# A decoder layer with its call list written anew: an earlier Exp table, a later broadcast, dummy products inside norm 2

## The chip, the core and the metric

The kernel runs on one core of a Trainium2 chip. The metric is the device time of one execution in microseconds (us). The engines are PE (TensorE: matmuls, with PEld for its weight loads), DVE (VectorE), ACT (ScalarE), POOL (GpSimd) and SP (SyncE, which here only issues transfers). Each engine runs its own list of instructions in the order in which the program wrote them; semaphores make one engine wait for another.

## The reference, cut to what matters

One decoder layer on 256 tokens of width 1024, all in float32:

```
mod = c @ w_ada + b_ada                      # sh1, sc1, g1, sh2, sc2, g2
h   = rmsnorm(x, norm1_g) * (1 + sc1) + sh1  # norm 1
q, k, v, xr, gr = split(h @ w_in)            # 5 x 512 columns
attn = attention(rmsnorm(q), rmsnorm(k), v)  # 8 heads, one causal block of 256
lru  = rg_lru(causal_conv4(xr)) * gelu(gr)   # gates, decay exp(-8 r softplus(-lambda)), scan over time
x = x + g1 * (concat(rmsnorm(lru), rmsnorm(attn)) @ w_out)
h2 = rmsnorm(x, norm2_g) * (1 + sc2) + sh2   # norm 2
gate, val = split(causal_conv3(h2 @ w_up))   # 2 x 2816 columns
x = x + g2 * ((silu(gate) * val) @ w_down)
```

## The kernel before, in words

Activations lie transposed: features on the 128 partitions, tokens along the row, so a 1024-wide tensor is 8 tiles (kt 0 to 7) of 128 x 256. Every large product is done three times on halves of the numbers: a weight w is cast to a high part wh (`hi`, L158, by default on ACT) and the rest wl = w - wh (`lo`, L167, on DVE), and h likewise to hh (`h_hi`, L387) and hl (`h_lo`, L390). The product is wh hh + wh hl + wl hh, so one weight tile needs four engine steps before PE has all of it.

Weights come in tiles of 1 MB, in the order of the list `order` (L101 to L113): g1 0, lin 0, g1 1, lin 1, then ada1 and lin in turn, v, g1 2 to 5 and wo, s2, g1 6 to 9, and up and dn. There are six buffers (NW = 6): when a tile has been used for the last time (`used`, L134), the next of the list is sent for (`send`, L117), and SP issues the transfers in that order. "g1" tiles hold columns of w_ada, which PE multiplies with c in 32-column products (`m1_mm`, `g1_mm`); "ada1", "s2" and "g2" tiles hold rows, which DVE multiplies with a broadcast copy of c (`ada`, L360; cb, L185).

The stages, in order:

- Head. PE runs dummy products of an identity matrix (`warm_up`, L224) while x arrives in four pieces. ACT squares it, DVE adds, PE sums over the partitions (`x_sum`), then comes 1/rms (`norm_s`, `norm_r`) and its spread over partitions (`norm_mm`). The modulation of kt 0 and 1 goes PE, ACT, PE, DVE (`m1_mm`, `m1_row`, `m1_col`, `m1_add`). `normed` and `h_hi` then make the first hh. `sp_act` and `sp(0)` to `sp(17)` (L333 to L357) are the softplus of lambda: Abs and Exp on ACT, then a series on DVE.
- lin. 8 tiles of w_in, with outputs x (RG-LRU), g (gelu), q and k. `lin(kt, out, i)` is output out with the i-th of the three products.
- Middle. The convolution (`conv_a`, `conv_d`), the RG-LRU (`gate`, `sigm`, `decay_a`, `decay_t`, `root`, `one_more`, `recur_u`, `recur_scan`, ...), the norms of q and k (`qk_r`), attention by head (`sc`, `s_max`, `s_exp`, `p_T`, `p_copy`, `pv`), and the v products as filler on PE. `v_copy` (L582) brings v out of PSUM; `pv` needs it.
- wo. `wo(c, kt)`, the output projection; then `res`, the sums of squares of norm 2 (`res_sq`, `res_add`, `res_sum`), 1/rms, `normed(1, kt)`, and the first `up`.
- up and down. `up(f, kt)`, `gated_*(f)`, `down(f, m)` for 22 panels f. From f = 4 a plain loop (L1443) writes them.

From the head to panel 3 the order on each engine is a list of some 640 calls written by hand (L801 to L1437): the scheduler is off, so a call's place in the list is its place in its engine's queue. `table(func)` (L220) is a call that does one element of a function, so that ACT loads that function's table there; without it the load comes with the first real use.

Of the kernel before, what the change touches and what calls it, by code (L numbers as in the profile page):

```python
# [13 lines left out]
P = 128  # L14
# [54 lines left out]
def hybrid_layer(ctx: ExitStack, tc: tile.TileContext, x_d, c_d, pk_d, bd_d, ada1_d, lin_d, v_d,  # L69
# [31 lines left out]
    order = []  # L101
# [4 lines left out]
    order += [("g1", 2), ("g1", 3), ("wo", 0), ("g1", 4), ("g1", 5), ("wo", 1)]  # L106
# [693 lines left out]
    kept.enter_context(tc.manual_schedule())  # L800
    warm_up(9)  # L801
    x_sq(0)
    x_sq(1)
    consts()
    c_cols()
    x_add(0, 1)
    x_sq(2)
    x_add(0, 2)
    x_sq(3)
    x_add(0, 3)  # L810
    table(AF.Sqrt)
    warm_up(12)
# [88 lines left out]
    ada("ada1", 1, 1)
    lin(2, "q", 2)
    lin(2, "g", 2)
    h_lo(0, 2)
    ada_add("ada1", 1)
    lin(2, "g", 0)
    lo("lin", 3, 0)
    normed(0, 3)
    sp(7)
    h_hi(0, 3)  # L910
    lin(2, "g", 1)
    lin(2, "x", 1)
    lin(2, "k", 1)
    lin(2, "q", 1)
    ada("ada1", 2, 0)
    h_lo(0, 3)
    lin(3, "g", 2)
    lin(3, "g", 0)
    ada("ada1", 2, 1)
    hi("lin", 4, 0)  # L920
    lo("lin", 3, 1)
    ada_add("ada1", 2)
    lin(3, "q", 0)
    normed(0, 4)
    lin(3, "k", 1)
    h_hi(0, 4)
    lin(3, "x", 2)
    lin(3, "x", 0)
    lin(3, "x", 1)
    lin(3, "g", 1)  # L930
    lin(3, "q", 2)
    sp(8)
    lo("lin", 4, 0)
    hi("lin", 4, 1)
    h_lo(0, 4)
    hi("lin", 5, 0)
    lin(3, "k", 2)
    lin(4, "x", 0)
    ada("ada1", 3, 0)
    lin(4, "g", 2)  # L940
    c_more(2)
    lin(4, "k", 1)
    lin(3, "k", 0)
    ada("ada1", 3, 1)
    lin(4, "x", 2)
    ada_add("ada1", 3)
    normed(0, 5)
    bd_load()
    lin(3, "q", 1)
    lo("lin", 4, 1)  # L950
    h_hi(0, 5)
    lin(4, "x", 1)
    h_lo(0, 5)
    lin(4, "q", 0)
    lin(4, "g", 0)
    lo("lin", 5, 0)
    hi("lin", 5, 1)
    ada("ada1", 4, 0)
    table(AF.Gelu_apprx_tanh)
    ada("ada1", 4, 1)  # L960
    lin(4, "k", 0)
    lin(5, "g", 0)
    lin(4, "g", 1)
    lin(5, "g", 1)
    hi("lin", 6, 0)
    lin(5, "k", 1)
    sp(9)
    ada_add("ada1", 4)
    lin(4, "q", 2)
    lin(5, "x", 1)  # L970
    sp(10)
    lin(5, "q", 1)
    lo("lin", 5, 1)
    lin(5, "x", 0)
    lin(5, "k", 0)
    lin(5, "q", 0)
    lin(4, "k", 2)
    normed(0, 6)
    lin(5, "g", 2)
    lin(5, "q", 2)  # L980
    lo("lin", 6, 0)
    h_hi(0, 6)
    h_lo(0, 6)
    ada("ada1", 5, 0)
    c_more(1)
    hi("lin", 6, 1)
    lin(5, "x", 2)
    table(AF.Exp)
    lin(6, "g", 0)
    ada("ada1", 5, 1)  # L990
    table(AF.Gelu_apprx_tanh)
    ada_add("ada1", 5)
    sp(11)
    normed(0, 7)
    lin(5, "k", 2)
    hi("lin", 7, 0)
    lin(6, "q", 0)
    sp(12)
    lin(6, "x", 0)
    lin(4, "q", 1)  # L1000
    lin(6, "q", 1)
    h_hi(0, 7, 1)
    lin(6, "g", 2)
    sp(13)
    hi("lin", 7, 1)
    lin(6, "g", 1)
    h_lo(0, 7)
    lin(6, "x", 2)
    lin(6, "k", 0)
    bd_copy(1)  # L1010
    lo("lin", 7, 0)
    lo("lin", 6, 1)
    lin(6, "x", 1)
    lin(7, "x", 1)
    lin(7, "x", 2)
    lin(7, "x", 0)
    lin(7, "q", 0)
    lin(7, "g", 1)
    bd_copy(0)
    lin(6, "q", 2)  # L1020
    conv_a(2)
    conv_a(0)
    lo("lin", 7, 1)
    conv_a(1)
    conv_a(3)
    hi("v", 0, 0)
    conv_d(0)
    lin(7, "q", 2)
    lin(7, "q", 1)
    lin(7, "k", 1)  # L1030
    lin(6, "k", 1)
    lin(7, "g", 2)
    q_s(0)
    q_s(1)
    q_sq(1)
    q_sq(0)
    c_more(3)
    lin(7, "g", 0)
    gelu(0)
    lin(7, "k", 0)  # L1040
    gelu(1)
    conv_d(1)
    lin(7, "k", 2)
    lin(6, "k", 2)
    k_sq(0)
    q_sum()
    k_sq(1)
    conv_d(2)
    conv_d(3)
    k_sum(0)  # L1050
    q_row(0)
    gate(1, 0)
    k_sum(1)
    q_col()
    sigm(1, 1)
    gate(0, 0)
    qk_r(0)
    gate(1, 1)
    sigm(0, 0)
    table(AF.Sigmoid)  # L1060
    sigm(1, 0)
    qk_r(1)
    lo("v", 0, 0)
    gate(0, 1)
    g1_mm(3)
    qk_r(2)
# [493 lines left out]
```

## Time and profile before

| | us |
|---|---|
| median of 3 runs (332.19 to 333.26) | 332.77 |
| the profiled execution | 332.59 |
| its span, first to last instruction | 330.8 |
| PE busy | 320.2 (97%) |
| DVE busy | 263.0 (79%) |
| ACT busy | 194.5 (59%) |

The profiled execution is 0.18 below the median, and 1.8 of it lie outside the span. A busy PE is a PE with some matmul in flight, not a PE at its peak; what ends the idle time before an instruction stands in brackets in the rows further on. The share of 97% is an average over stages: from the fourth panel on PE never waits, and the stages before are those in which other engines can hold it up.

### The profile page before, as it was taken

Reading aid. Unit: us, or ns where it says so; the run is one execution under the profiler, and the core shown is the slowest. Engines: PE = TensorE matmul, PEld = TensorE weight load, DVE = VectorE, ACT = ScalarE, POOL = GpSimd, SP = SyncE. Lnnn points to the kernel's source line nnn. Section 1 sums busy time; section 2 is a strip of 40 time slices with the busy share of each in tenths; the row PEclk is TensorE's granted clock in tenths of the full one; section 3 lists DMA queues with packets and bytes.
Section 4 is the critical chain, followed back from the end, with each engine's and each line's share of the span. In section 5 each row is a group of like instructions: output and inputs, shape, how many; then the busy total and the mean of one; then the engine's idle time right before and its main releaser. Section 6 shows DMA issues by size and latency. Waiting matters only on the chain.

```text
span 330.8 us, 6467 instructions
## 1 busy us (share of the span) xinstructions
PE 320.2 (97%) x2608; PEld 302.6 (91%) x2608; DVE 263.0 (79%) x507; ACT 194.5 (59%) x328; POOL 4.6 (1%) x22
## 2 busy tenths in 40 slices
PE   7899999999999999899999999999999999999994
PEld 7789999767599996899999999999999999999994
DVE  2469999899999998968696788888888677685654
ACT  5635458999988245865566455464646464655520
POOL 5000000000000000000000000000000000000000
PEclk9999999999999999799999999999999999999998
DMA  7999999939355998836566557575849463300003
GB/s 224 337 405 408 410 408 422 411 136 385 131 162 206 345 407 316 348 129 254 167 223 248 174 214 264 206 293 183 323 146 364 135 242 133 129 0 2 3 0 127
DMA packets 18013, 77.89 MB, mean 235 GB/s; under 512 B 1600, under 2 KB 6336, under 8 KB 10944
## 3 DMA queue, kind: packets, MB, share of 16 engines
q1 hardware_dynamic: 17840, 77.34, 62.6%
q8 instruction: 20, 0.33, 0.4%
q10 hardware_dynamic: 144, 0.15, 0.2%
q14 instruction: 9, 0.07, 0.1%
HBM read 76.43 MB, written 1.05 MB: 234 GB/s over the span
## 4 chain that ended last, share of the span: by engine, by line
PE 69%; DVE 16%; ACT 6%; issue 3%; SPq 2%; DMA 2%; DVEq 0%; ACTq 0%
PE bank L65 68%; DVE wl L172 4%; DVE w L365 4%; DMA w<-in_dram 2%; DVE m L423 2%; ACT wh L144 1%; SPq L132 1%; DVE m L766 1%; PE bank L676 1%; DVE ht L381 1%; ACT p L670 1%; DVE m L794 1%; DVE m L458 1%; DVE wh L150 1%; SPq L181 1%
## 5 line engine op out<-in xcount | busy, mean ns | idle before, releaser
L172 DVE TENSOR_TENSOR wl<-w,wh 128x1024 fp32r<-128x1024 f32 x94 | 113.2, 1220 | 19.8 <-ACT wh L144 19.1
L144 ACT CAST wh<-w 128x1024 fp32r<-128x1024 f32 x90 | 92.1, 1043 | 43.6 <-PE bank L65 34.9
L65 PE MATMUL bank<-hh__1575,wh 128*128 128x256 f32 x352 | 71.6, 285 | 1.1 <-ACT hh__1575 L148 1.1
L65 PE MATMUL bank<-hl__1576,wh 128*128 128x256 f32 x352 | 71.7, 286 | 0.0
L65 PE MATMUL bank<-hh__1575,wl 128*128 128x256 f32 x352 | 71.6, 285 | 0.0
L65 PEld LDWEIGHTS bank<-hh__1575,wh 128*128 128x128 f32 x352 | 55.3, 193 | 1.3 <-ACT hh__1575 L148 1.3
L65 PEld LDWEIGHTS bank<-hl__1576,wh 128*128 128x128 f32 x352 | 55.6, 194 | 0.2 <-DVE hl__1576 L392 0.2
L65 PEld LDWEIGHTS bank<-hh__1575,wl 128*128 128x128 f32 x352 | 55.4, 194 | 0.2 <-DVE wl L172 0.2
L766 DVE SCALAR_TENSOR_TENSOR m<-bank,pk,m 128x255 f32<-128x255 f32 x88 | 40.4, 479 | 19.0 <-ACT m L758 17.4
L65 PE MATMUL bank<-pl,wh 128*128 128x256 f32 x176 | 49.9, 284 | 0.4 <-DVE pl L782 0.4
L65 PE MATMUL bank<-ph,wh 128*128 128x256 f32 x176 | 49.9, 284 | 0.0
L65 PE MATMUL bank<-ph,wl 128*128 128x256 f32 x176 | 49.8, 283 | 0.0
L65 PEld LDWEIGHTS bank<-pl,wh 128*128 128x128 f32 x176 | 33.8, 192 | 0.6 <-DVE pl L782 0.6
L65 PEld LDWEIGHTS bank<-ph,wh 128*128 128x128 f32 x176 | 33.8, 192 | 0.1
L65 PEld LDWEIGHTS bank<-ph,wl 128*128 128x128 f32 x176 | 33.8, 192 | 0.0
L758 ACT ACTIVATE m<-bank,pk 128x256 f32<-128x256 f32 x44 | 22.4, 558 | 18.9 <-PE bank L65 18.9
L365 DVE CUSTOM_DVE_ANT_0 w<-w,cb 128x1024 f32<-128x1024 f32 x22 | 26.3, 1218 | 0.0
L770 ACT ACTIVATE m<-m 128x256 f32<-128x256 f32 x22 | 9.2, 417 | 26.8 <-DVE m L766 26.8
L65 PE MATMUL bank<-hl_mix__1178,wh 128*128 128x256 f32 x64 | 18.3, 286 | 0.2 <-DVE hl_mix__1178 L505 0.2
L65 PE MATMUL bank<-hh_mix__1177,wh 128*128 128x256 f32 x64 | 18.4, 288 | 0.0
L65 PE MATMUL bank<-hh_mix__1177,wl 128*128 128x256 f32 x64 | 18.1, 283 | 0.0
L65 PE MATMUL bank<-hh__245,wh 128*128 128x256 f32 x96 | 14.8, 283 | 1.0 <-DVE lt L345 1.0
(176 smaller groups left out, 429.5 us busy)
## 6 DMA issues: line engine op xcount, KB each, us to landing
w<-in_dram SPq DMA_DIRECT2D x55, 1024.0 KB, 5.1
w<-in_dram SPq DMA_DIRECT2D x32, 512.0 KB, 10.1
xT<-in_dram SPq DMA_DIRECT2D x4, 256.0 KB, 4.5
cb<-in_dram SPq DMA_DIRECT2D x1, 512.0 KB, 9.7
out_dram<-m SPq DMA_DIRECT2D x4, 128.0 KB, 2.5
out_dram<-m SPq DMA_DIRECT2D x2, 256.0 KB, 2.8
m<-in_dram SPq DMA_DIRECT2D x1, 256.0 KB, 9.5
pk<-in_dram ACTq DMA_DIRECT2D x1, 145.0 KB, 4.0
```

The source lines that it names most:

```text
L65: self.nc.tensor.matmul(out, lhsT, rhs, start=left == self.n, stop=left == 1, skip_group_check=True)
L132: (q or nc.sync).dma_start(raw[key][:, c:c + n], srcs[key[0]][key[1]][:, c:c + n])
L144: nc.scalar.copy(out, in_)
L150: nc.vector.tensor_copy(out, in_)
L172: (nc.vector if e else nc.gpsimd).tensor_sub(l[:, c], raw[key][:, c], h.bitcast(F32)[:, c])
L181: nc.sync.dma_start(xT[:, 2 * i:2 * i + 2, :], x_d[:, 2 * i:2 * i + 2, :])
L365: nc.vector.tensor_tensor_reduce(v[:, a, :], v[:, a, :], cb, scale=scale, scalar=0.0, op0=ALU.mult, op1=ALU.add, accum_out=mod[:, j, kt:kt ...
L381: nc.vector.scalar_tensor_tensor(T["ht", n, kt], xT[:, kt, :], mod[:, (SC1, SC2)[n], kt:kt + 1], rep, op0=ALU.mult, op1=ALU.mult)
L423: nc.vector.scalar_tensor_tensor(xc[:, t, s:], pair(B["x", t // 2])[:, t % 2, :S - s], col(O_CW + 4 * j + t), xc[:, t, s:], op0=ALU.mult, ...
L758: nc.scalar.activation(cv[:, s, :], pair(B["up", f])[:, s, :], AF.Identity, scale=col(O_FW + 88 + i), bias=col(O_FB + i))
L766: nc.vector.scalar_tensor_tensor(cv[:, s, d:], pair(B["up", f])[:, s, :S - d], col(O_FW + 44 * j + i), cv[:, s, d:], op0=ALU.mult, op1=ALU ...
L770: nc.scalar.activation(T["cv", f][:, 2, :], T["cv", f][:, 0, :], AF.Silu)
```

## The change

Six edits and a new order.

1. ACT loads the Exp table before anything else, and `sp_act` runs as soon as the packed parameters are there, ahead of the squares of x; `sp(0)` to `sp(5)` follow on DVE ahead of the adds. The Sqrt table is loaded after the squares, as before.
2. The dummy products: 18 in one run before `x_sum` in place of 21, and 3 in place of 8 behind it. sc1's column (`m1_row`, `m1_col`, `m1_add` of part 0) is taken before sh1's products (`m1_mm(0, 1)`) are made.
3. c's broadcast is sent for after the fourth weight tile (lin 1) and not after the third.
4. g1 4 and g1 5 come ahead of wo 0 in the list of weights.
5. `keep_warm`: 5 dummy products whose result nobody reads, in two places between the sums of norm 2 and the first `up`. Beside them, `g1_mm(6)`, `(7)` and `(9)` come before the last sums and `(8)` after.
6. Some casts change engine: for example `h_hi(1, 2)` and both casts of up 4 go from ACT to DVE, and the second cast of wo 2 and one of v 0 from DVE to ACT.

The calls themselves, but for the dummy products and the `table` calls, are the same ones; lines behind L226 move by 7.

```diff
-    order += [("g1", 2), ("g1", 3), ("wo", 0), ("g1", 4), ("g1", 5), ("wo", 1)]
+    order += [("g1", 2), ("g1", 3), ("g1", 4), ("g1", 5), ("wo", 0), ("wo", 1)]
...
     for i in range(NW):
         send()
-        if i == 2:
+        if i == 3:
             nc.sync.dma_start(cb, c_d.to_broadcast([P, D]))
...
+    def keep_warm(n):
+
+        b = get(B, "idle", lambda: bank(3, 1))
+        for _ in range(n):
+            b.reopen(1)
+            b.mm(b.t[:, 0:P], ident, ident)
...
+    table(AF.Exp)
     warm_up(9)
+    sp_act()
     x_sq(0)
+    consts()
+    sp(0)
...
     norm_s("n2")
+    g1_mm(8)
+    keep_warm(2)
     g1_row(1)
     norm_r()
     g1_col(1)
+    norm_mm("n2")
+    keep_warm(3)
     lo("up", 1, 0)
-    norm_mm("n2")
     g1_add(1)
     normed(1, 2)
-    h_hi(1, 2)
+    h_hi(1, 2, 1)
```

Three places show how the lists move. The first is PE in the head, before; ident are the dummy products (and, with rms, the spread of 1/rms), ccol the columns of c, ones the column sums, and hh with wh the first product of lin:

```order
L65 MATMUL bank_147<-ident 128x128 x21
L65 MATMUL bank_185<-ones,m_157 128x2 x4
L65 MATMUL bank_199<-w,ccol 32x128 x8
L65 MATMUL bank_147<-ident 128x128 x6
L65 MATMUL bank_199<-w,ccol 32x128 x8
L65 MATMUL bank_185<-ident,rms 128x128 x2
L65 MATMUL bank_199<-ones,m_230 128x2
L65 MATMUL bank_199<-ones,m_232 128x2
L65 MATMUL bank_147<-ident 128x128 x2
L65 MATMUL bank_253<-hh__245,wh 128x256 x2
```

The same place on PE in the changed kernel:

```order
L65 MATMUL bank_148<-ident 128x128 x18
L65 MATMUL bank_191<-ones,m_160 128x2 x4
L65 MATMUL bank_205<-w,ccol 32x128 x8
L65 MATMUL bank_148<-ident 128x128
L65 MATMUL bank_205<-ones,m_214 128x2
L65 MATMUL bank_205<-w,ccol 32x128 x8
L65 MATMUL bank_191<-ident,rms 128x128 x2
L65 MATMUL bank_205<-ones,m_232 128x2
L65 MATMUL bank_148<-ident 128x128 x2
L65 MATMUL bank_253<-hh__243,wh 128x256 x2
```

Three dummy products before the sums and five behind them are gone, and one column sum stands ahead of the second group of ccol products.

The second place is ACT in the attention, before, from the first exponential on; p are the probabilities, L465 the squares of the RG-LRU output, pt copies a transposed head, m_1041 is v:

```order
L670 ACT_TABLE_LOAD
L670 ACTIVATE p,rs<-p,eb,iqk 128x128
...
L465 ACTIVATE m_885<-m_784 128x1024
L144 COPY pt<-bank_1008 128x384
...
L144 COPY m_1041<-bank_862 128x512
L144 COPY pt<-bank_1029 128x384
L144 COPY m_1041<-bank_898 128x512
```

The same stretch of ACT in the changed kernel (m_1044 is v, the casts are the two halves of wo 0's high part):

```order
L677 ACT_TABLE_LOAD
L677 ACTIVATE p,rs<-p,eb,iqk 128x128
L677 ACTIVATE p,rs<-p,eb,iqk 128x256
L144 CAST wh<-w 128x1024
...
L472 ACTIVATE m_869<-m_754 128x1024
...
L144 COPY m_1044<-bank_848 128x512
L222 ACTIVATE warm<-ones 128x1
L144 COPY row<-bank_877 128x256
L144 COPY pt<-bank_1022 128x384
L144 COPY m_1044<-bank_837 128x512
```

Before, three heads' exponentials (two rows each) stand ahead of the second copy of v; now four heads', two casts and a row copy do, while the three casts that came ahead of the table load are gone.

The third place is DVE at norm 2, before; sr are the sums of squares, xT<-bank the residual adds, hm and rms the norm, ht the first normed tiles:

```order
L740 TENSOR_TENSOR sr<-sr 128x256 x5
L732 SCALAR_TENSOR_TENSOR xT<-bank_1421,mod,xT 128x256 x2
L172 TENSOR_TENSOR wl<-w,wh 128x1024
L375 TENSOR_TENSOR mod<-mod,pk 128x2 x2
L172 TENSOR_TENSOR wl<-w,wh 128x1024
L375 TENSOR_TENSOR mod<-mod,pk 128x2
L273 TENSOR_SCALAR hm<-bank_1502 128x2
```

The same place on DVE in the changed kernel:

```order
L739 SCALAR_TENSOR_TENSOR xT<-bank_1410,mod,xT 128x256 x2
L747 TENSOR_TENSOR sr<-sr 128x256 x2
L172 TENSOR_TENSOR wl<-w,wh 128x1024
L150 CAST wh<-w 128x1024
L172 TENSOR_TENSOR wl<-w,wh 128x1024
L280 TENSOR_SCALAR hm<-bank_1521 128x2
```

Between the last residual adds and hm there are now two adds, two splits and a cast of up 1's second half, where there were two splits of up 0 and three small adds.

## Rows read from the trace of the kernel before

**Rows 1.** The page: busy times of the engines, and the granted clock over the span.
```profile
PE 320.2 (97%) x2608; PEld 302.6 (91%) x2608; DVE 263.0 (79%) x507; ACT 194.5 (59%) x328; POOL 4.6 (1%) x22
...
PEclk9999999999999999799999999999999999999998
```
**Rows 2.** PE's waits: line, waited for, total us, times, longest us.
```profile
PE bank L65 <- ACT hh__1575 L148: 1.1, 1, 1.1
...
PE bank L65 <- DVE pl L782: 0.4, 1, 0.4
```
**Rows 3.** Stretches: length; busy us of each engine; clock; DMA share; GB/s.
```profile
64.40:100.20 35.80, 35.03 (x262) 26.07 (x263) 34.14 (x102) 33.47 (x80) 0.00 (x0) 1.00 0.57 217
...
133.20:137.00 3.80, 3.77 (x17) 3.55 (x18) 3.79 (x10) 2.67 (x6) 0.00 (x0) 0.55 1.02 427
```
**Rows 4.** Timeline of the head: start us, length us, instruction, idle before it.
```profile
1.75 7.54 PE L65 MATMUL bank<-ident 128*128 128x128 f32 x42 [1.75 <-POOL ident L197]
...
6.50 1.37 ACT L305 ACTIVATE m<-xT 128x512 f32<-128x512 f32 x2 [0.44 <-DMA xT<-in_dram]
...
10.12 0.26 ACT L268 ACTIVATE rms<-bank,eps 128x2 f32<-128x2 f32 x1 [0.73 <-PE bank L65]
...
10.58 1.60 PE L65 MATMUL bank<-ident 128*128 128x128 f32 x12
...
14.37 0.48 DVE L381 SCALAR_TENSOR_TENSOR ht<-xT,mod,bank 128x256 f32<-128x256 f32 x1
...
15.45 0.71 PE L65 MATMUL bank<-hh__245,wh 128*128 128x256 f32 x4 [0.97 <-DVE lt L345]
```
**Rows 5.** Transfers issued in 4.1 to 4.3 us: KB, us to landing.
```profile
w<-in_dram SPq DMA_DIRECT2D x1, 512.0 KB, 8.1
```
**Rows 6.** Transfers issued in 8.4 to 9 us.
```profile
w<-in_dram SPq DMA_DIRECT2D x1, 512.0 KB, 10.1
```
**Rows 7.** Timeline early in the lin stage, PE.
```profile
19.50 0.65 PE L65 MATMUL bank<-w,ccol 128*32 128x128 f32 x16
```
**Rows 8.** Timeline at the end of the lin stage, ACT, DVE and PE.
```profile
52.25 1.28 ACT L222 ACT_TABLE_LOAD   x1
...
56.23 3.50 DVE L172 TENSOR_TENSOR wl<-w,wh 128x1024 fp32r<-128x1024 f32 x3
...
58.77 1.93 ACT L148 ACTIVATE m<-bank,pk 128x256 f32<-128x256 f32 x4 [0.34 <-PE bank L65]
...
64.90 0.64 PE L65 MATMUL bank<-m,sel 128*32 128x256 f32 x8 [0.50 <-ACT m L436]
```
**Rows 9.** Timeline of the middle, ACT and PE.
```profile
77.09 1.06 ACT L449 ACTIVATE m<-m 128x1024 f32<-128x1024 f32 x1
...
83.97 0.49 ACT L670 ACTIVATE p<-p,eb,iqk 128x128 f32<-128x128 f32 x1 [0.73 <-DVE eb L665]
...
89.33 0.58 ACT L144 COPY m<-bank 128x512 f32<-128x512 f32 x1
...
90.44 0.88 PE L65 MATMUL bank<-m,pt 128*128 128x64 f32 x6
...
100.22 0.37 PE L65 MATMUL bank<-hh_mix__1177,wh 128*128 128x256 f32 x1
```
**Rows 10.** Timeline of norm 2, PE.
```profile
126.39 1.93 PE L65 MATMUL bank<-w,ccol 128*32 128x256 f32 x32
128.41 1.05 PE L65 MATMUL bank<-ones,sr 128*128 128x2 f32 x8
...
131.42 0.69 PE L65 MATMUL bank<-ident,rms 128*128 128x128 f32 x4
133.23 0.58 PE L65 MATMUL bank<-hh__1575,wh 128*128 128x256 f32 x2 [1.11 <-ACT hh__1575 L148]
...
134.77 0.63 PE L65 MATMUL bank<-hh__1575,wh 128*128 128x256 f32 x2
```
**Rows 11.** Transfers issued in 118.1 to 118.2 us.
```profile
w<-in_dram SPq DMA_DIRECT2D x1, 1024.0 KB, 9.6
```

More of the change, by code (lines that the diff above doesn't have):

```diff
@@ new lines, in hybrid_layer @@
+    ada_add("ada1", 1)
+    lin(2, "k", 1)
+    sp(13)
+    normed(0, 3)
+    h_hi(0, 3)
+    lin(2, "q", 0)
+    lin(2, "q", 2)
+    lo("lin", 3, 0)
+    lin(2, "g", 1)
+    h_lo(0, 3)
+    ada("ada1", 2, 0)
+    ada("ada1", 2, 1)
+    ada_add("ada1", 2)
+    hi("lin", 3, 1)
+    lo("lin", 3, 1)
+    lin(2, "x", 2)
+    hi("lin", 4, 0)
+    lin(2, "k", 2)
+    lin(2, "k", 0)
+    lin(2, "g", 2)
+    normed(0, 4)
+    lin(2, "q", 1)
+    lin(3, "x", 0)
+    lin(3, "x", 2)
+    lo("lin", 4, 0)
+    lin(3, "q", 0)
@@ L917, in hybrid_layer @@
+    h_hi(0, 4)
+    h_lo(0, 4)
+    hi("lin", 4, 1)
+    ada("ada1", 3, 0)
+    hi("lin", 5, 0)
+    lin(3, "k", 0)
     lin(3, "g", 2)
+    ada("ada1", 3, 1)
+    bd_load()
+    lin(3, "g", 1)
+    lin(3, "k", 1)
     lin(3, "g", 0)
[L919 to L928, printed above, removed]
     lin(3, "x", 1)
-    lin(3, "g", 1)
+    lo("lin", 4, 1)
+    lin(3, "q", 1)
@@ L931, in hybrid_layer @@
     lin(3, "q", 2)
[L932 to L936, printed above, removed]
+    ada_add("ada1", 3)
     lin(3, "k", 2)
     lin(4, "x", 0)
-    ada("ada1", 3, 0)
-    lin(4, "g", 2)
[L941 to L955, printed above, removed]
@@ L981, in hybrid_layer @@
-    lo("lin", 6, 0)
+    lin(4, "x", 2)
+    lin(4, "k", 0)
+    lin(4, "q", 1)
+    normed(0, 5)
+    h_hi(0, 5)
+    lo("lin", 5, 0)
+    lin(4, "k", 1)
+    h_lo(0, 5)
+    ada("ada1", 4, 0)
+    lin(4, "g", 0)
+    lin(4, "q", 0)
+    lin(4, "x", 1)
+    ada("ada1", 4, 1)
+    hi("lin", 5, 1)
+    lin(4, "g", 2)
+    lin(4, "q", 2)
+    sp(15)
+    hi("lin", 6, 0)
+    ada_add("ada1", 4)
+    normed(0, 6)
+    lin(4, "g", 1)
+    lo("lin", 5, 1)
     h_hi(0, 6)
     h_lo(0, 6)
+    hi("lin", 6, 1)
@@ L1026, in hybrid_layer @@
[L1026 to L1042, printed above, removed]
     lin(7, "k", 2)
     lin(6, "k", 2)
+    conv_a(3, 1)
+    gelu(1)
+    conv_a(1)
+    conv_a(2)
+    table(AF.Sigmoid)
+    lin(7, "k", 1)
+    conv_d(0)
+    q_sq(1)
+    lin(7, "k", 0)
+    conv_d(2)
+    conv_d(1)
@@ new lines, in hybrid_layer @@
+    gated_d(1, 0)
+    up(2, 3)
+    up(2, 5)
+    up(2, 7)
+    gated_d(0, 1)
+    gated_d(1, 1)
+    gated_s(0)
+    gated_m(0)
+    gated_s(1)
+    table(AF.Sqrt)
+    hi("dn", 0, 1, 1)
+    gated_m(1)
+    up(3, 6)
+    up(3, 4)
+    gated_h(0)
+    hi("dn", 0, 0)
+    up(3, 7)
+    table(AF.Exp)
+    gated_l(0)
+    lo("dn", 0, 0)
+    up(2, 6)
+    up(2, 2)
+    hi("up", 4, 0, 1)
+    up(3, 5)
+    up(3, 0)
+    down(0, 3)
+    gated_h(1)
+    table(AF.Silu)
+    up(3, 2)
+    gated_l(1)
```

786 lines of the change are left out of this document (368 added, 418 removed).

## The prediction, made before the changed kernel had run

> **What bounds the kernel now.** I read the page first: PE is busy for 97% of the span, DVE 79%, ACT 59%, and the granted clock is full but for one digit, a 7, a little before the middle [rows 1]. So time can come from three places only: moments when PE has nothing, work on PE that goes away, and a stretch where its clock is low. PE's waits came next. From norm 2 on there are two, 1.1 us before the first `up` and 0.4 before the first `down` [rows 2]; in the plain loop behind, PE waits for nothing. The end therefore moves with the first `up` matmul (133.23 [rows 10]), plus what the clock takes behind it and that last 0.4. Then the stretches: in 133.2 to 137.0 the clock is 0.55, and in the middle, 64.4 to 100.2, PE is busy 35.0 of 35.8 us but DVE 34.1 and ACT 33.5 as well [rows 3]. There three engines bound each other, so a gain on one is easily lost. Last I read the timeline of the head, the end of lin, the middle and norm 2 [rows 4, 7, 8, 9, 10] and the landing times of three transfers [rows 5, 6, 11].
>
> The profiled execution, 332.59, stands 0.18 below the median of 332.77; terms are made against it and 0.18 is added at the end.
>
> **A. Head: 2.0 us earlier.** Before, the dummy products end at 1.75 + 7.54 = 9.29 and 1/rms's root starts 0.83 later, at 10.12; the squares of x end at 7.87, held by x's transfer [rows 4]. 18 products instead of 21 take away 6 records of 42, 1.1 us at their mean, so the sums then hang on the squares and an add (0.7 to 0.9, estimate), 8.7: the root goes to 9.6 to 9.85, and I take 9.85, 0.27 earlier. Behind it 5 of 8 dummy products go, 10 of 12 records in 1.60 [rows 4], 1.33 us of PE that stands in the way of the spread. sc1's column, which `ht` needs, is taken before sh1's products: 0.4 by my estimate (one row copy and one column that are no longer last). Together 2.0: `ht` at 12.35 for 14.37, and with the same 1.08 behind it the first lin product at 13.4 for 15.45. Cover: lin 0's first half, issued at 4.1 at the latest 4.3, lands at about 12.2 [rows 5], and its cast (1.06, as ACT's root over the same tile [rows 9]) ends at 13.3. Without that cover the gain would stop there, so A can't be more than 2.1. `sp_act` and `sp` ahead of the squares use ACT and DVE while x is in flight; the extra cost if they ran late would be at most a table load, 1.28 [rows 8].
>
> **B. Lin: 1.5 left.** g1 1's second half, issued at 8.4, lands at 18.5 [rows 6], whatever the head does. Before, PE came to the products that need it at 19.50 and did not wait [rows 7]. Now they stand ahead of five products of lin 0, and PE reaches them sooner: seven groups of four matmuls at 0.48 (estimate from 0.71 for the first four with their fill [rows 4]) from 13.4 to 16.8, the first eight ccol products to 17.4, a wait of 1.1 to 18.5, the other eight 0.6, a row copy 0.35 and the column sums 0.35 (both estimates), 19.8; then six groups to 22.7. Before, the same thirteen groups, products and sums from 15.45 on take 13 x 0.48 + 2 x 0.65 [rows 7] and some 1.1 for the sums and the changing between them (estimate), 24.1. The lead of 2.0 is 1.5 here; bounds 0.7 (the row copy late and no changing saved) and 2.0. c's broadcast, 2.5 us later for a 1 MB tile at 427 GB/s [rows 3], is needed by `ada` about 1 us after it lands. Two table loads with their dummy elements (1.28 each [rows 8]) go from ACT ahead of lin's last casts; `conv_a` moves from 58.77 to about 57.5 and PE's first q sum, which waits 0.50 at 64.90 [rows 8], comes at about 63.4.
>
> **C. Middle: 1.4 of it given back.** From `conv_a` to `root` ACT has one weight cast more (+1.06, the price of the root [rows 9]), one convolution copy less (−0.48, a quarter of 1.93 [rows 8]) and smaller waits; `root` is 0.9 early, ending at 77.25 for 78.15 [rows 9]. The first exponential doesn't follow it at once: even before, it waited 0.73 for DVE's `eb` [rows 9], and DVE's list is as long. From there to the second copy of v ACT now has one head's exponentials more (0.49 and about 0.58), casts moved in from ahead of the Exp load, a row copy (0.36, estimate), and one earlier cast less (−1.06). I get v copied at 89.9, where it ended at 89.91 before, `pv(0)` at 90.1 for 90.44, and the first wo product at 100.1 for 100.22 [rows 9]. So I forecast that nearly all of the head's gain ends here. Bounds: 98.7 (all of 1.5 kept) to 101.5 (three more ACT steps of 0.4 to 0.5 ahead of v). I take the value near the low end of the gain because ACT and DVE have only 2.3 and 1.7 us free in 35.8 [rows 3].
>
> **D. wo and norm 2: −0.8 in all, C's −0.1 included.** `g1_mm(6)` (0.95, and about 0.35 for changing over) leaves the wo stretch, so wo ends 1.4 earlier, near 124.4. Then PE has three g1 products (32 records of two took 1.93 [rows 10]; 2.9), three sums (1.5, from 1.05 for two), `g1_mm(8)` 0.95, two dummy products, the g1 column, and the spread, which ends near 131.0; before, it stood at 131.42 to 132.11 [rows 10]. DVE adds, splits and casts up to `hm` at 129.1, then `lo(up, 1, 0)`, 1.17 as one of the three splits [rows 8], ends at about 131.0. `g1_add`, `normed` and `h_hi` take 1.4; `h_hi` on DVE instead of ACT saves a change of engine (0.3). The first `up` comes at 132.4 for 133.23. Bounds 131.4 (DVE's splits hidden) to 134.0 (both splits after the inverse in the way).
>
> **E. Clock: −1.5.** Before, 3.8 us at 0.55 did the work of 2.1 at the full 2.4 GHz, so 1.7 are lost [rows 3]; three pairs from 133.23 to 134.77 take 0.51 each [rows 10], where two matmuls at 0.12 to 0.18, a quarter of B's 0.48 and of the first four's 0.71, would take 0.24 to 0.36. What PE did ahead of the fall: products of 0.95, sums, then two short spells in the last 2 us and a wait of 1.11 [rows 10]. In the new order PE is busy from 124.4 to about 131.7 with some 0.7 idle. I take 1.5 of the 1.7, bounds 0 and 1.7. The Trainium skill, "TensorE: Matmul & The Clock Gate", section "Why this matters for your kernels", has it that short gaps don't cost the clock, only long spells of PE idle. By that rule a wait of 1.1 would have cost nothing, dummy products would bring nothing, and the forecast would be 331.7. The trace of before disagrees: its longest idle before the fall is 1.11 and the clock is 0.55 behind it; so the measurement decides, and the rule stands as the first rival.
>
> **F. First panels: −0.3.** The 0.4 before the first `down` [rows 2] goes, since more `up` groups lie behind `gated_a(0)`; small stalls at the first `up` products (up to 0.1) come in.
>
> **Sum.** −0.8 (A to D as it arrives at the first `up`) −1.5 −0.3 = −2.6: 332.59 − 2.6 = 330.0, with 0.18 330.2. Its own range is 329.2 to 331.4.
>
> **Rivals.**
> 1. The clock falls all the same. For it: DVE still has splits between the sums and the first `up`, and PE's dummies are short; a single late step on DVE would leave PE idle for 1 us again. Against: nearly all of those 8 us are filled. Only −0.8 and −0.3 stay: 331.7.
> 2. The head's lead goes through to wo. For it: the two loads gone from lin free ACT, and PE waits for it there; against it ACT and DVE at 93 and 95% in the middle [rows 3]. Then wo begins 1.4 sooner than forecast, at 98.7: 330.2 − 1.4 = 328.8.
> 3. up 1 lands late, and that makes it slower. In before it was issued at 118.1 and took 9.6, so 127.7 [rows 11]. Now DVE's cast of it stands ahead of `hm`, needs it by about 127.3, and queued behind it are the split, `hm`, `normed` and all that PE waits for. I estimate the issue at 119.4, since the buffer is freed by a split of wo 3 that comes later: landing at 129.0, 1.7 late, takes 331.9 at the full clock. With one more 1 MB tile ahead of it (2.5 us at 427 GB/s [rows 3]) it lands at 131.5, 4.2 late: 334.4. It is slower than before from a landing at about 130.9 on. For it: 427 GB/s is what the queue moved at its fastest here. Against: at 118 that traffic had left off, and before it took 9.6 for a whole tile.
>
> **Chances.** Forecast 0.48, clock falls 0.21, head kept 0.14, up 1 late 0.17 (of which 0.05 comes out near 331.9 and 0.12 slower). This kernel's measurement can tell 0.3%, 1.0 us, from no change: faster is below 331.8, slower above 333.8. Faster: the forecast, the kept head, and a small part (0.04) of the clock's rival, which at 331.7 lies on the bound: 0.66. Same: the rest of that rival and the mild late tile, 0.22. Slower 0.12. The range 328.4 to 333.2 takes in the kept head down to 0.4 below its price and the clock's rival up to 1.5 above its own (D's upper bound); it leaves out the slow case.
>
> **What will show it.** A: the first lin product at 13.4. B: PE waits some 1 us before g1 1's second products, and q's first sum comes at 63.4. C: root ends near 77.25, but wo begins near 100.1; a start at 98.7 makes rival 2 right. D: first `up` at 132.4, waiting for DVE. E: clock 1.00 in the 4 us behind it; 0.5 makes rival 1 right. F: no wait before the first `down`. Rival 3: DVE's cast of up 1 waits for a transfer. The forecast is wrong if the first `up` comes after 133.2, or if in the plain loop PE waits anywhere.

## The result, and the profile after

The changed kernel takes 330.76 us (median of 8 runs) where the kernel before takes 332.41: a ratio of 0.9929, 95% interval [0.9907, 0.9952]. Three of the 8 runs took 336 us and more; such runs came here, in a_nokeep (2 of 12) and in h_baa (3 of 12) and in no other kernel, they are left out of the ratios and of the medians further on, and no trace shows what they lost. The other five have a median of 330.50 and fall in two groups: 329.38 and 329.58 with a mean granted clock of 1.00, and 330.50, 330.73 and 330.79 with 0.991 to 0.992. The profiled run, 330.79, is of the second group.

The page of the changed kernel, as in [rows 1]:

```profile
PE 318.0 (97%) x2602; PEld 301.3 (92%) x2602; DVE 268.9 (82%) x517; ACT 190.0 (58%) x320; POOL 4.6 (1%) x22
...
PEclk9999999999979999999999999999999999999998
```

The 7 is still there, but it has moved, from slice 17 (norm 2) to slice 12, which begins at 90.5 us. Three stretches of the changed kernel (columns as in [rows 3]) show both places:

```profile
88.00:91.60 3.60, 2.72 (x24) 2.20 (x21) 3.46 (x16) 3.60 (x12) 0.00 (x0) 1.00 0.01 5
91.60:95.00 3.40, 3.40 (x19) 2.48 (x16) 1.75 (x12) 2.53 (x8) 0.00 (x0) 0.50 0.70 241
133.80:137.60 3.80, 3.80 (x30) 3.64 (x31) 3.58 (x10) 3.00 (x5) 0.00 (x0) 1.00 1.01 423
```

Behind the first `up`, where [rows 3] has 0.55 and 17 matmuls, the clock is 1.00 and PE does 30. In the attention PE is busy for 2.72 of 3.60 us and then runs at 0.50 for 3.4 us; in the kernel before PE was busy throughout the same 3.6 us. PE's two waits in it are short:

```profile
88.88 0.58 PE L65 MATMUL bank<-ones,m 128*128 128x2 f32 x4 [0.45 <-DVE m L477]
...
90.17 1.33 PE L65 MATMUL bank<-m,pt 128*128 128x64 f32 x10 [0.43 <-ACT m L144]
```

The first is for the squares of the RG-LRU output, the second for ACT's second copy of v.

Norm 2 of the changed kernel on PE, beside [rows 10]:

```profile
125.70 2.80 PE L65 MATMUL bank<-w,ccol 128*32 128x256 f32 x48
128.43 1.50 PE L65 MATMUL bank<-ones,sr 128*128 128x2 f32 x12
129.86 1.07 PE L65 MATMUL bank<-w,ccol 128*32 128x256 f32 x16
130.86 0.71 PE L65 MATMUL bank<-ident 128*128 128x128 f32 x4
131.42 0.61 PE L65 MATMUL bank<-sel,row 128*128 128x4 f32 x4
131.89 0.69 PE L65 MATMUL bank<-ident,rms 128*128 128x128 f32 x4
132.41 0.83 PE L65 MATMUL bank<-ident 128*128 128x128 f32 x6
133.80 0.47 PE L65 MATMUL bank<-hh__1573,wh 128*128 128x256 f32 x2 [0.56 <-DVE mod L382]
```

The first `up` comes 0.57 later than before (133.80 for 133.23), and the end of the span still 1.8 earlier (329.0 for 330.8). So 2.4 us are won behind the first `up`, and 0.6 lost ahead of it. This table of the profiled runs shows where (start of the first lin product, of the first column sum of q, end of ACT's root, start of the first wo, up and down products, end of the span):

| kernel | lin | q sum | root ends | wo | up | down | end |
|---|---|---|---|---|---|---|---|
| before | 15.45 | 64.90 | 78.15 | 100.22 | 133.23 | 153.98 | 330.8 |
| changed | 14.22 | 62.88 | 77.55 | 101.03 | 133.80 | 154.98 | 329.0 |
| difference | −1.23 | −2.02 | −0.60 | +0.81 | +0.57 | +1.00 | −1.8 |

Times of the head differ from profile to profile of the same list: the first lin product comes at 14.83 to 15.53 in the five profiles with the head of before, and at 13.80 to 14.22 in the four with the changed head in which the clock stayed full there. So a few tenths at one stage of one pair of profiles say little. Lengths between two stages repeat better where neither the clock nor the weights interfere: from wo to `up` it takes 32.99 to 33.02 in five profiles with the list of before, and 32.77 to 32.79 in six with that of the changed kernel.

### The profile page after: what moved, and what is told of

The parts are those of the page before. It is cut to its first block, busy times and chain, and to the rows that moved or that the text cites. A ratio compares the mean times of both kernels' runs of the same rounds, so it can differ in the third digit from the quotient of the medians.

```text
span 329.0 us, 6457 instructions
## 1 busy us (share of the span) xinstructions
PE 318.0 (97%) x2602; PEld 301.3 (92%) x2602; DVE 268.9 (82%) x517; ACT 190.0 (58%) x320; POOL 4.6 (1%) x22
## 4 chain that ended last, share of the span: by engine, by line
PE 80%; ACT 9%; DVE 7%; DMA 1%; issue 1%; DVEq 0%; ACTq 0%
PE bank L65 80%; ACT p L677 2%; DVE wl L172 2%; DMA pk<-in_dram 1%; ACT wh L144 1%; ACT pt L144 1%; DVE m L801 1%; DVE m L315 1%; PE bank L683 1%; ACT m L449 1%; ACT m L452 0%; ACT m L148 0%; ACT m L144 0%; ACT L456 0%; ACT L449 0%
## 5 line engine op out<-in xcount | busy, mean ns | idle before, releaser
L144 ACT CAST wh<-w 128x1024 fp32r<-128x1024 f32 x87 | 89.7, 1043 | 40.9 <-PE bank L65 32.9
L65 PEld LDWEIGHTS bank<-hh__1573,wh 128*128 128x128 f32 x352 | 54.9, 192 | 0.7 <-PE bank L65 0.7
L65 PEld LDWEIGHTS bank<-hl__1574,wh 128*128 128x128 f32 x352 | 54.9, 192 | 0.2 <-DVE hl__1574 L399 0.2
## 6 DMA issues: line engine op xcount, KB each, us to landing
w<-in_dram SPq DMA_DIRECT2D x32, 512.0 KB, 10.1
```

The source lines that it names most:

```text
L65: self.nc.tensor.matmul(out, lhsT, rhs, start=left == self.n, stop=left == 1, skip_group_check=True)
L144: nc.scalar.copy(out, in_)
```

## The experiments

Each kernel ran beside the kernel before, whose median lay at 332.67 to 332.76 in the four groups of runs. Times are medians of a kernel's runs unless single ones are named; a stage's times are those of its one profile.

**1. The dummy products of norm 2, away and alone.**

a_nokeep, from the changed kernel:

```diff
     g1_mm(8)
-    keep_warm(2)
     g1_row(1)
...
     norm_mm("n2")
-    keep_warm(3)
     lo("up", 1, 0)
```

> The changed kernel without the five dummy products of norm 2 (nothing else reads them). Theory (the clock falls behind a spell in which PE idles, and the dummies prevent it): the granted clock is 0.5 to 0.55 for 3 to 4 us behind the first up product, and the end comes 1.2 to 1.7 us later than with them, near 332.2. Rival (gaps of 1 us cost no clock, as the rule on long gaps has it): the clock stays at 1.00 there and the time at 330.7.

Measured 331.50, ten runs between 330.51 and 333.44; ratio 0.9979 [0.9955, 1.0002]. That is 1.0 above the changed kernel's 330.50, and the two intervals against the kernel before do not overlap; the theory said 1.2 to 1.7, the rival nothing. In its profile PE waits twice in norm 2, 0.49 for the row of g1 and 1.06 before the first `up`, where the changed kernel waits once, 0.56. The clock fell at 131.6, behind the first of the two, and stayed at half until 138.4:

```profile
131.15 0.61 PE L65 MATMUL bank<-sel,row 128*128 128x4 f32 x4 [0.49 <-ACT row L144]
131.61 1.20 PE L65 MATMUL bank<-ident,rms 128*128 128x128 f32 x4
133.87 0.76 PE L65 MATMUL bank<-hh__1567,wh 128*128 128x256 f32 x2 [1.06 <-DVE mod L382]
```

```profile
12.40:15.70 3.30, 3.30 (x16) 3.19 (x17) 2.25 (x7) 2.86 (x5) 0.00 (x0) 0.52 1.15 300
131.70:133.80 2.10, 1.11 (x5) 0.82 (x4) 1.59 (x7) 0.00 (x0) 0.00 (x0) 0.50 0.99 414
133.90:137.60 3.70, 3.70 (x17) 3.70 (x18) 3.48 (x10) 2.93 (x5) 0.00 (x0) 0.50 1.01 423
```

From the first `up` to the end it takes 196.93 where the changed kernel takes 195.20 (329.0 − 133.80): 1.73 more, and from the first wo product to the end 2.07 more. So the wait of 1.06 did not bring the fall here; it came behind the fall and may owe part of its length to it, since the spread of 1/rms takes 1.20 instead of 0.69. The first stretch was not expected either: in this run the clock also fell in the head, which is the same as the changed kernel's.

b_keep, from the kernel before:

```diff
     norm_s("n2")
+    keep_warm(2)
     g1_row(1)
...
     norm_mm("n2")
+    keep_warm(3)
     g1_add(1)
```

> The kernel before with the same five dummy products put into its norm 2 (two behind the last g1 product, three behind the spread of 1/rms), nothing else changed. Theory: clock 1.00 in 133.2 to 137.0 where it was 0.55, first up still near 133.2, end 1.5 earlier, 330.9. Rival: the dummies alone do not hold the clock, since the order around them is the old one with PE idle between them: clock 0.5 to 0.6 there, time within 0.3 of 332.4.

Measured 331.04, all 12 runs between 330.74 and 331.44; ratio 0.9970 [0.9951, 0.9989]. The stretch that answers to [rows 3], and its first `up`:

```profile
132.90:136.70 3.80, 3.76 (x29) 3.55 (x30) 3.79 (x10) 2.67 (x6) 0.00 (x0) 1.00 1.00 416
```

```profile
132.93 0.51 PE L65 MATMUL bank<-hh__1581,wh 128*128 128x256 f32 x2 [0.45 <-ACT hh__1581 L148]
```

The dummies alone hold the clock; from `up` to the end 197.57 becomes 196.17, so 1.4. They remove a spread, too: of the 35 runs of the kernel before in this group, 9 took 330.58 to 331.17 at a clock of 0.996 or more and the other 26 took 332.14 to 333.87 at 0.995 or less. The fall comes in about three runs of four, and the dummies bring all runs to the level of the nine. The rival of a_nokeep, that idle of about 1 us costs no clock, is out.

**2. The fall in the attention.** a_mid, from the changed kernel (`mid_warm` is `keep_warm` on a free bank):

```diff
+    mid_warm(2)
     lru_sum()
...
+    mid_warm(2)
     pv(0)
```

> The changed kernel with four more dummy products in the attention, two ahead of the column sums of the RG-LRU output and two ahead of the first pv, where PE idles 0.45 and 0.43 us. Theory (the clock fell to 0.50 in 91.6 to 95 because PE had idled just before, and that is why wo begins at 101.0 and not at 100.1): clock 1.00 there, wo begins near 99.9, end 1.1 earlier than the profiled run of the changed kernel: 329.5, in every run. Rival: the dummies only push pv back by 0.3 to 0.5 and the clock falls all the same: 330.9 to 331.2.

Measured 329.82; ratio 0.9934 [0.9910, 0.9959]. Nine of 12 runs lie between 329.38 and 329.92. The two stretches of its profile, now full and at 1.00, and its first wo:

```profile
88.00:91.60 3.60, 3.60 (x32) 3.31 (x33) 3.42 (x17) 3.60 (x12) 0.00 (x0) 1.00 0.00 0
91.60:95.00 3.40, 3.19 (x31) 2.72 (x29) 2.56 (x18) 3.40 (x10) 0.00 (x0) 1.00 0.84 282
```

```profile
99.62 0.37 PE L65 MATMUL bank<-hh_mix__1170,wh 128*128 128x256 f32 x1
```

Root ends at 77.13 here, so root to wo is 22.49, for 23.48 in the changed kernel's profile: the fall cost 0.99. The theory fits this profile, but not "every run": one took 330.51, and two, at 332.18 and 332.80 with a clock of 0.989, had lost more. Nor does the profile alone show that the dummies did it. a_dummy, further on, has no dummies in the attention and the same two gaps (0.45 and 0.43), and its profile kept the clock:

```profile
88.00:91.60 3.60, 2.72 (x23) 2.18 (x23) 3.50 (x15) 3.60 (x13) 0.00 (x0) 1.00 0.04 14
91.60:95.00 3.40, 3.19 (x29) 2.56 (x28) 2.56 (x16) 3.40 (x10) 0.00 (x0) 1.00 0.62 173
```

So did a_nokeep's in the attention. What speaks for the four dummies is the count of runs: with them (a_mid, a_fill, a_fill4) 23 of 30 runs have a clock of 0.996 or more, without them (changed kernel, a_dummy, h_baa) 12 of 26. These kernels differ in the head too, so this makes the theory likely and does not show it.

**3. The head.** b_dummy, from the kernel before:

```diff
-    warm_up(12)
+    warm_up(9)
     x_sum()
...
-    warm_up(2)
     sp(0)
-    warm_up(4)
+    warm_up(1)
```

> The kernel before with the dummy products of the head cut as in the changed kernel: 18 for 21 ahead of the sums, 1 for 6 behind. Theory (the middle is bound by ACT and DVE and gives back what the head wins): first lin product at about 13.9 for 15.45, some 0.6 lost where g1 1's second half has not landed yet, and at wo at most 0.3 left; time 332.1 to 332.5. Rival: the lead goes through, 331.0 to 331.4.

Measured 332.40; ratio 0.9995 [0.9973, 1.0018]. The first lin product comes at 14.20, as early as in the changed kernel, but q's sum only at 64.73 and wo at 100.06: of 1.25 us won, 0.17 are left after lin. Between 22 and 25 us PE now waits 0.21 for a cast and 0.42 for a split of weights, which it did not before. So the old lin stage gives the lead back, not the middle; the g1 products did not wait for their weights. b_keep, whose head is that of before and happened to be 0.62 early, agrees: 0.31 of it is left at q's sum and at wo.

a_dummy, from the changed kernel, is the reverse:

```diff
-    warm_up(9)
+    warm_up(12)
     x_sum()
...
     m1_row(0, 0)
-    warm_up(1)
+    warm_up(6)
```

> The changed kernel with as many dummy products in the head as before (21 ahead of the sums of x, 6 for 1 behind them). Theory (in the new order the chain from the first lin product to root is rigid, 63.33 us in each profile, while the old order took up 1.1 of the 1.25 in its lin stage): first lin product at 15.2 to 15.4, root ends 1.0 to 1.2 later, at 78.6, and the runs at clock 1.00 are at 330.4 to 330.7 for 329.4 to 329.6. Rival (new order too has slack behind the head): root ends within 0.3 of 77.5, those runs at 329.4 to 329.8.

Measured 330.65; ratio 0.9958 [0.9935, 0.9982]. The lower eight of 12 runs are at 330.20 to 330.72. First lin product at 14.79, root ends at 78.08: 63.29 between them, for 63.33 in the changed kernel and in a_mid and 63.36 in h_abb. Its sums happened to start early (8.79 for 9.10), so the lead lost is 0.57 and not 1.0; all of it arrives. In the new order lin hands a lead on us for us, in the old one hardly.

**4. The order of the stages, by hybrids.** Each takes its calls from one list up to a point and the rest from the other; the place of c's broadcast goes with the head, and the order of the weights (edit 4) with the middle. h_abb: changed up to the end of lin, then before.

```diff
     k_sq(0)
-    gate(0, 0)
-    gate(1, 0)
+    q_s(1)
     k_sq(1)
...
```

> Head and lin in the changed order (with c's broadcast after the fourth tile), everything from the norms of q on in the order before, no dummy products in norm 2. Theory M (the new order of the middle is itself 1.8 us longer from the first q sum to wo, 37.16 for 35.32; a lead is passed on there us for us): q sum at about 62.9, wo at 98.2, 2.0 earlier than before, time near 330.7. Rival S (my step C: ACT and DVE bound the middle and swallow the lead whatever the order): wo near 100.0, time near 332.4.

Measured 332.38; ratio 1.0006 [0.9980, 1.0031]. q sum at 62.68, root ends at 77.38, wo at 99.46. Neither theory's number: of 2.2 won at q's sum 0.77 are left at root, also with the old order of the middle, and these arrive at wo whole (root to wo 22.08, as before's 22.07). So the lead is eaten between lin and root, and the rows show where: ahead of DVE's convolution. Its first steps before, in h_abb and in the changed kernel (the number of records depends on the window asked for):

```profile
60.28 3.85 DVE L423 SCALAR_TENSOR_TENSOR m<-bank,pk,m 128x255 f32<-128x255 f32 x8 [0.55 <-ACT m L148]
```

```profile
59.44 4.75 DVE L430 SCALAR_TENSOR_TENSOR m<-bank,pk,m 128x255 f32<-128x255 f32 x10 [0.25 <-ACT m L148]
```

```profile
59.63 4.76 DVE L430 SCALAR_TENSOR_TENSOR m<-bank,pk,m 128x255 f32<-128x255 f32 x10 [0.25 <-ACT m L148]
```

From there to the end of root it takes 17.87, 17.94 and 17.92, so a lead of 0.84 or 0.65 at the convolution is what root gets. In the new lin order q's sum comes earlier against the convolution than in the old (3.25 us behind its start for 4.62), which is why the lead looked like 2 us at q's sum. ACT is not busier on the way: it works 18.50 of the 20.00 us from its first convolution copy to the end of root in h_abb, and 18.76 of 19.38 before.

h_baa: before up to the end of lin, then changed.

```diff
     conv_d(3)
-    k_sum(0)
-    q_row(0)
+    sp(15)
+    sp(16)
+    gate(0, 0)
...
```

> Head and lin in the order before, everything behind in the changed order, with the dummy products of norm 2. Theory M: q sum at 64.6 to 64.9, wo 37.2 later (102), 1.8 later than before; with 1.6 from the clock, 1.0 from the first panels and 0.2 from norm 2 the time is near 331.6. Rival S: wo at 100.2, time near 329.9.

Measured 332.38, from 330.84 to 335.34; ratio 1.0008 [0.9977, 1.0039]. Two runs at a clock of 1.00 took 330.84 and 331.38. In the profiled one the clock fell in the attention for twice as long as in the changed kernel:

```profile
90.00:100.00 10.00, 9.11 (x52) 7.62 (x50) 7.06 (x35) 7.79 (x21) 0.00 (x0) 0.66 0.29 107
```

Root ends at 79.53 and wo starts at 104.60, 25.07 later. As a test of M against S this run says little, since the fall covers it; it does say that the new attention is where the clock is at risk, whatever lies ahead.

h_bba: before up to the last wo products, then changed.

```diff
     hi("up", 0, 0)
-    res_add(5)
+    ada_add("s2", 3)
+    ada_add("s2", 2)
+    g1_mm(9)
     res(7)
...
```

> The order before up to the last wo products, from there (norm 2, first panels) the changed one with its dummy products. Steps D, E and F alone. As in the prediction: norm 2 0.7 shorter, clock 1.5, first panels 0.3: 330.2 against 332.7. As the runs so far suggest: norm 2 0.2 shorter, clock 1.6, first panels 1.0 (no wait at the first down): 329.9, clock 1.00 behind the first up in every run.

Measured 330.65, all 9 runs between 330.06 and 331.79; ratio 0.9941 [0.9921, 0.9961]. Norm 2 and the first panels alone bring what the whole change brings. From `up` to the end 195.18, as in the changed kernel; from wo to `up` 33.41, longer than either (33.01 and 32.77); at this cut two g1 products stand in new places, and whether they are the cause was not tried. The rest of the change thus adds next to nothing to the median: the 1 us that it is worth in the two runs of the changed kernel at a clock of 1.00 (329.38 and 329.58 against 330.65) is lost in the other three.

h_aba: changed, then before in the middle, then changed.

```diff
     k_sq(0)
-    gate(0, 0)
-    gate(1, 0)
+    q_s(1)
...
     hi("up", 0, 0)
-    res_add(5)
+    ada_add("s2", 3)
...
```

> Changed order in head and lin and again from norm 2 on, the order before in between (norms of q to wo). Theory M: wo at 98.2, no wait at the first down, clock 1.00 everywhere: 327.8, 1.7 below the changed kernel's best runs. Rival S: 329.5 or above, since the middle swallows the lead of 2.

Measured 330.18, 6 runs between 329.95 and 331.06; ratio 0.9931 [0.9905, 0.9957]. Theory M is out: wo at 100.18. In this profile lin itself took 49.52 to q's sum where h_abb, the same program up to there, took 48.66; ACT waited 13.4 us for weights in all, for 8.4. Why the weights came later in this run is open.

**5. The wait before the first down.** b_keep_down, from b_keep:

```diff
+    up(2, 2)
+    up(3, 0)
     down(0, 4)
...
-    up(2, 2)
...
-    up(3, 0)
```

> The kernel before with the dummy products in norm 2, and with up(2, 2) and up(3, 0) moved ahead of the four first down calls. Theory (the wait of 0.43 before the second down product costs PE 0.6, and that is most of what the changed kernel wins behind the first up): no such wait, end 0.5 to 0.7 earlier than with the dummies alone, 330.4 for 331.04. Rival (the wait hides something else that then shows, and the new gain there has another source): 330.9 to 331.1.

Measured 330.50 (330.25 to 330.91 in 12 runs); ratio 0.9950 [0.9930, 0.9971]. The first two down products of b_keep, then of b_keep_down:

```profile
152.28 0.28 PE L65 MATMUL bank<-ph,wh 128*128 128x256 f32 x1
152.99 0.38 PE L65 MATMUL bank<-pl,wh 128*128 128x256 f32 x1 [0.43 <-DVE pl L789]
```

```profile
154.09 0.28 PE L65 MATMUL bank<-ph,wh 128*128 128x256 f32 x1
154.21 0.28 PE L65 MATMUL bank<-pl,wh 128*128 128x256 f32 x1
```

A wait shown as 0.43 costs 0.71 − 0.12 = 0.59: it is counted from the end of the matmul before it, 0.28 after that one's start, while without a wait the next starts after 0.12. From `up` to the end 196.17 becomes 195.51, 0.66 less.

**6. The fall in the head.** a_fill, from a_mid:

```diff
-    warm_up(9)
+    warm_up(11)
     x_sum()
...
     norm_c()
-    warm_up(2)
+    warm_up(3)
```

> The changed kernel with the four dummy products in the attention, and three more in the head where PE idles (20 for 18 ahead of the sums of x, 3 for 2 ahead of lin). Theory (what is left of the spread of times is the clock falling behind idle spells of PE, in the head too): first lin product within 0.3 of 14.2, clock 1.00 throughout, every run between 329.3 and 330.1, median 329.7. Rival (the falls have another cause): a spread of over 1.5 us as without the three.

Measured 329.57; ratio 0.9939 [0.9911, 0.9967]. Eight of 12 runs at 329.33 to 329.76, but three at 330.86 to 332.36. The profiled run is one of those; the sums of x, and two stretches of its head:

```profile
9.00 1.05 PE L65 MATMUL bank<-ones,m 128*128 128x2 f32 x8 [1.14 <-DVE m L322]
```

```profile
7.90:9.00 1.10, 0.00 (x1) 0.01 (x1) 1.04 (x3) 1.10 (x1) 0.00 (x0) 1.00 1.16 313
11.30:18.20 6.90, 6.59 (x42) 6.08 (x43) 4.49 (x13) 4.87 (x7) 0.00 (x0) 0.51 1.09 347
```

The 20 dummies were done by 7.85; then PE stood still for 1.1 us, and from 11.3 on the clock was half for 6.9 us. Root ends at 79.95, 2.4 later than in the changed kernel, and all of it arrives at the end (330.4, where a_fill4 below, without a fall, ends at 328.0).

a_fill4, as a_fill but with 22 dummies:

```diff
-    warm_up(11)
+    warm_up(13)
     x_sum()
```

> As the changed kernel with the dummy products in the attention and 3 ahead of lin, and now 22 for 18 ahead of the sums of x: in the profile with 20 they had ended at 7.85 and PE idled 1.14 us before the sums, and the clock was 0.50 from 11.3 to 18.2. Theory (an idle of about 1 us there lets the clock fall): the idle is under 0.6, clock 1.00 through the head, first lin product at 14.0 to 14.6, every run between 329.3 and 330.4. Rival (the falls of the head do not hang on that idle): a run or more in twelve above 331.5, as with 20.

Measured 329.94, 5 of 6 runs at 329.75 to 330.08 and one at 331.15; ratio 0.9921 [0.9903, 0.9939]. In its head PE does not wait for the sums:

```profile
1.74 7.63 PE L65 MATMUL bank<-ident 128*128 128x128 f32 x44 [1.74 <-POOL ident L197]
9.21 0.95 PE L65 MATMUL bank<-ones,m 128*128 128x2 f32 x8
```

The clock is 1.00 through the head and the whole profile, and the first lin product comes as early as in the changed kernel (14.23). No run was above 331.5, but six runs are few, and one at 0.995 shows that a fall is still possible. a_mid, a_fill and a_fill4 lie below both kernels in their medians; their intervals against the kernel before overlap the changed kernel's, so that they are faster than it is likely from the spread of the runs and not shown by the ratios.

## Why the prediction was right, and which steps were not

The forecast was 330.2, the result 330.76: faster, by 0.7%. The largest term, the clock behind the first `up`, holds with its reason. The rest of the sum is partly luck: A to D brought 0.4 at the first `up` in place of 0.8, F brought 1.0 in place of 0.3, and a fall of the clock that was not foreseen took about 1 back. By one of its own signs the forecast was wrong, since the first `up` came at 133.80, after 133.2; without the fall it comes at 132.82 (a_fill4).

**A, head: mis-sized, 1.23 for 2.05.** The five dummies behind the sums are worth 0.85 to 0.88, not 1.33: from the sums to the first lin product it takes 6.32 before and 5.47 in b_dummy, 6.00 in a_dummy and 5.12 in the changed kernel. The other 0.35 between b_dummy and the changed kernel may be sc1's column (0.4 in the step). The start of the sums, which the step put at 8.7, brought nothing: they came at 9.10, as before (9.13), though for another reason. Before, the dummies end at 9.29 and hold them; now DVE's last add does. For that the step had no term: it took `sp` ahead of the squares as filling time while x is in flight. DVE's adds before, then the packed parameters' arrival and the adds in the changed kernel:

```profile
7.17 1.49 DVE L308 TENSOR_TENSOR m<-m,m 128x512 f32<-128x512 f32 x2 [0.47 <-ACT m L305]
```

```profile
5.20 0.24 DVE L244 SCALAR_TENSOR_TENSOR pk<-pk 128x8 f32<-128x8 f32 x2 [5.20 <-DMA pk<-in_dram]
...
6.76 1.49 DVE L315 TENSOR_TENSOR m<-m,m 128x512 f32<-128x512 f32 x2
...
8.35 0.69 DVE L315 TENSOR_TENSOR m<-m,m 128x512 f32<-128x512 f32 x1
```

Before, DVE waits for ACT's squares and ends its adds at 8.66. Now `sp(0)` to `sp(5)` stand between the parameters' arrival and the adds, DVE works through without a wait, and the last add ends at 9.04. In all eight profiles with this order it ends 3.84 to 3.90 behind the arrival, at 8.64 to 9.04; in the six with the old order it ends at 8.35 to 8.73. The sums, and two rows of the lin stage for the next step:

```profile
9.10 1.05 PE L65 MATMUL bank<-ones,m 128*128 128x2 f32 x8 [0.93 <-DVE m L315]
...
17.73 1.08 PE L65 MATMUL bank<-w,ccol 128*32 128x128 f32 x32
...
19.52 0.61 PE L65 MATMUL bank<-ones,m 128*128 128x2 f32 x4 [0.71 <-DVE m L150]
```

Taking the three dummies away can open an idle in front of the sums. It was 0.6 to 1.1 us in four of the six profiles of this head with 18 or 20 dummies (changed kernel, a_mid, a_nokeep, a_fill). That is a cost the step did not see: in two of the four (a_nokeep, a_fill) the clock fell 2.4 to 3.3 us behind it.

**B, lin: the wait did not come, and the lead was larger at q's sum.** The step had PE wait 1.1 us for g1 1's second half, to land at 18.5. In the rows above PE does all 32 of its products at 17.73 without a wait; the wait is 0.71 for a row copy on DVE, where I had put 0.35 and 0.35 for copy and sums. The mistake was to take the 10.1 us to landing [rows 6] as fixed. In the changed kernel the same half, issued at about 8.5, took 8.7 and landed near 17.2:

```profile
w<-in_dram SPq DMA_DIRECT2D x1, 512.0 KB, 8.7
```

c's broadcast no longer follows it in the queue, which may be the reason: the half took 8.7 to 10.1 in the six profiles with the broadcast behind it and 8.6 to 9.2 in the eight without. The ranges overlap, and no run tried that alone. From the first lin product to q's sum the new order takes 48.66 for 49.45. So the lead at q's sum was 2.0, not 1.5 (1.4 by the step's own 24.1 and 22.7). To the start of the convolution, on which root hangs, the new order takes longer, 45.41 for 44.83.

**C, middle: the amount right, the place not, and a clock fall missed.** Root ended 0.60 earlier (0.9 forecast), and h_abb shows that the lead is lost ahead of DVE's convolution, with either order of the middle; the step had it lost on ACT's work from `conv_a` on. From root to wo the new order is 0.42 longer (22.49 in a_mid and a_dummy for 22.07). Without a fall wo begins at 100.03 in a_fill4, whose first lin product is at 14.23 as in the changed kernel; the step said 100.1. What failed is that the step priced ACT's list and did not ask what PE's two gaps of 0.45 and 0.43 us ahead of pv can do to the clock. The fall behind them cost 0.99 in the profile, and 1.2 between the two groups of runs (329.5 and 330.7).

**D, norm 2: mis-sized, 0.24 for 0.7.** From wo to `up` it takes 32.77; the forecast's 132.4 − 100.1 is 32.3, and before it was 33.01. DVE came to `hm` at 130.46, 0.43 later than the step's 129.1 moved by the late wo. From `ht` to `up` it takes 1.01 for 1.08, so the change of engine saved by `h_hi` on DVE is nearer 0.1 than the step's 0.3. up 1's weights were not late, and rival 3 is out: DVE's cast of up 1 follows the split of up 0 with no idle between.

```profile
127.46 1.22 DVE L172 TENSOR_TENSOR wl<-w,wh 128x1024 fp32r<-128x1024 f32 x1
128.60 0.69 DVE L150 CAST wh<-w 128x1024 fp32r<-128x1024 f32 x1
```

**E, clock: right.** 1.5 forecast; 1.4 from before to b_keep. The longer fall of a_nokeep cost 1.73 behind `up`. The step overlooked one wait: in the kernel before, too, PE waits 0.49 for the row of g1 in norm 2, 1.2 us ahead of the 1.11, and a_nokeep's clock fell behind this one.

```profile
130.95 0.61 PE L65 MATMUL bank<-sel,row 128*128 128x4 f32 x4 [0.49 <-ACT row L144]
```

Which of the two brought the fall before is not shown; the five dummies fill both. The Trainium skill's rule in "TensorE: Matmul & The Clock Gate", "Why this matters for your kernels", that only long idle costs clock, does not agree with these runs. The clock was at half behind waits of 0.49 and 1.11 (before), of 0.49 (a_nokeep) and of 0.45 and 0.43 (attention).

**F, first panels: mis-sized, about 1.0 for 0.3.** b_keep to the changed kernel, from `up` to the end: 196.17 − 195.20 = 0.97, of which 0.66 is the wait before the second down product (b_keep_down) and the rest small stalls. I had put down the wait as printed and taken stalls off it that were there before as well.

With the right sizes and no fall in the attention the differences to before are, stage by stage: −1.23 at lin, −2.02 at q's sum, −0.60 at root, −0.2 at wo, −0.4 at `up` (the last two in a_fill4), and 2.4 more behind it: −2.8. The two runs of the changed kernel at a clock of 1.00 have spans of 327.6 and 327.8, 3.1 under before's 330.8; the three others lose 1.2 of that in the attention.

## What to carry to other kernels

After a change that shortens a queue, look for the places where PE now idles in several short pieces, and not at the longest wait alone: a gain of a microsecond ahead can cost the clock behind it, and a few matmuls that nobody reads held it in most runs here. Look at more than one run, too: one profile shows one of two outcomes. A wait printed on PE can cost more than its print (0.59 for 0.43 here). A lead won early in a program should be followed to the step that the next stage hangs on, here the start of DVE's convolution, before it is counted. And work moved ahead into waiting time is free only as long as the wait outlasts it.

## What the runs showed of the hardware

The granted clock went to half, 1.2 of 2.4 GHz, behind spells in which PE had idled: two waits of 0.49 and 1.11 us in norm 2 before, 0.49 alone in a_nokeep's norm 2, 1.1 at once in the head of a_nokeep and a_fill, two waits of 0.45 and 0.43 in the attention. The length of a wait does not decide it: the clock stayed at 1.00 behind 0.97 in the head of before, 0.93 in that of the changed kernel and 0.89 in front of h_bba's first `up`, and behind the same 0.45 and 0.43 in a_dummy. What else decides is not shown. The low stretch lasted 3.4 us in five places (norm 2 of before, b_dummy and h_abb, the changed kernel's attention, a_nokeep's head) and 6.8 in three (a_fill's head, a_nokeep's norm 2, h_baa's attention). One program takes a fall in one run and not in the next: 26 of 35 runs for norm 2 before, three of five for the attention after, both by the mean clock of the run. A short fall cost 1.0 to 1.4 us at the end, a long one 2.1 to 2.6.
